# Holding back the first store of an add-and-GELU kernel until chunk 19 is done

## The chip, the cores and the metric

One NeuronCore of a Trainium2 chip. The metric is the device time of one execution in microseconds (us), lower is better. The profile is of one execution; its span is shorter than the timed number by about 1.8 us (119.9 against 121.73 in the execution that was profiled), so spans are compared with spans and times with times. Engines have short names here: POOL is GpSimd, ACT ScalarE, DVE VectorE, and SP is SyncE, which issues the DMA transfers.

## The reference

```python
batch, dim = 1024, 4096                      # float32
z = x + y
return 0.5 * z * (1 + np.tanh(np.sqrt(2 / np.pi) * (z + 0.044715 * z ** 3)))
```

Two inputs of 16.8 MB are read, one output of 16.8 MB is written: 50.33 MB for very little arithmetic.

## The kernel before

On chip the data is one tile `z` of 128 partitions by 32,768 columns. It receives x by DMA; y comes into two rotating buffers of 8,192 columns. The work goes in 32 chunks of 1,024 columns: an addition (POOL, `add`), a square (ACT, `sq`), a multiply-add (DVE, `stt`), a sigmoid (ACT, `sig`) and a product (DVE, `mul`), which puts the result back into `z`. Loads and stores are large, and all are issued from one queue, SP's, with the stores after all loads:

```python
    loads = [2048, 6144, 8192, 8192, 8192]
    stores = [8192, 8192, 8192, 4096, 4096]
    ...
    def store(i):
        a, b = sr[i]
        nc.sync.dma_start(out=ov[:, a:b], in_=zt[:, a:b])
    ...
    def mul(c):
        a, b = cr[c]
        nc.vector.tensor_mul(out=zt[:, a:b], in0=wt[c], in1=zt[:, a:b])

    sp = []
    for i in range(len(loads)):
        sp += [(load_x, i), (load_y, i)]
    sp += [(store, i) for i in range(len(stores))]
    ...
        store: lambda i: [(mul, c) for c in over(cr, *sr[i])],
```

So a store waits for the products of its own columns (the first for chunk 7), and is issued when SP has issued everything ahead of it in this list.

## Time and profile before

| | before |
|---|---|
| time, median of the first three runs | 122.09 us |
| span of the profile | 119.9 us |
| DMA queue busy, share of 16 engines | 98.4% |
| DVE / ACT / POOL busy | 75.5 / 63.8 / 73.0 us |
| first and second store issued | 60.52 and 66.83 us |
| last load lands / last store lands | 80.67 / 119.67 us |

Two more belong here. The first is SP's line in the view of waits (what waited, for whom: us in total, times, the longest), the second the timeline of SP from 60.6 to 67.5 (start, duration, what):

```profile
SPq L131 <- DVE z L157: 41.8, 4, 19.4
```

A landing is the issue's start plus the time to landing of the DMA view. "Landing" is of the last of the 16 DMA engines. A DMA engine moves a transfer in packets, here mostly of 32 KB and 1.21 us each. The packet records behind the DMA view give start, duration and size, but not the engine. They show that the packets of an engine follow each other without a gap while it has work, so the last two load packets of the 16 engines are the last 32 of the load.

### The profile page before, as it was taken

What the parts mean: (1) busy time and instruction counts of PE and PEld (TensorE: products, weight loads), DVE (VectorE), ACT (ScalarE), POOL (GpSimd) and SP (SyncE); (2) the same over time, 40 slices, a digit from 0 to 9 for tenths busy, and PEclk for the clock granted to TensorE, in tenths of its full rate; (3) what the DMA queues carried; (4) which work ended last, traced back from release to release, by engine and by line L of the source; (5) the groups of instructions that cost most, each with busy time, mean ns of one, the idle gap of its engine ahead of it and who ended that gap; (6) DMA issues with size and microseconds to landing.
All of it is one profiled execution on the core that took longest, in us unless ns stands there. A gap on an engine that the chain in (4) does not pass through costs nothing.

```text
span 119.9 us, 247 instructions
## 1 busy us (share of the span) xinstructions
DVE 75.5 (63%) x66; ACT 63.8 (53%) x66; POOL 73.0 (61%) x35
## 2 busy tenths in 40 slices
DVE  0044700049999109999996999996899999600000
ACT  4006300078876038788867887884888887200000
POOL 0046000699990199999969999959999991000000
DMA  6999999989898999999898989999998989998995
GB/s 191 424 478 410 476 426 394 514 361 514 361 503 372 481 394 448 426 426 448 383 492 372 503 350 514 361 383 481 388 481 372 492 383 481 394 470 366 437 426 224
DMA packets 2162, 50.35 MB, mean 420 GB/s; under 512 B 240, under 2 KB 240, under 8 KB 240
## 3 DMA queue, kind: packets, MB, share of 16 engines
q1 hardware_dynamic: 2160, 50.33, 98.4%
q14 instruction: 2, 0.02, 0.0%
HBM read 33.55 MB, written 16.78 MB: 420 GB/s over the span
## 4 chain that ended last, share of the span: by engine, by line
DMA 49%; POOL 17%; DVE 16%; SPq 1%; ACT 1%; issue 0%; POOLq 0%
DMA y<-in_y_dram 49%; POOL z L137 17%; DVE z L157 8%; DVE w L148 8%; ACT w L142 1%; SPq L120 1%; SPq L127 1%; POOLq L137 0%
## 5 line engine op out<-in xcount | busy, mean ns | idle before, releaser
L137 POOL TENSOR_TENSOR z<-z,y 128x1024 f32<-128x1024 f32 x31 | 72.8, 2388 | 26.1 <-DMA y<-in_y_dram 26.1
L142 ACT ACTIVATE w<-z 128x1024 f32<-128x1024 f32 x32 | 32.9, 1028 | 37.3 <-POOL z L137 31.3
L148 DVE SCALAR_TENSOR_TENSOR w<-w,z 128x1024 f32<-128x1024 f32 x32 | 39.4, 1233 | 21.0 <-ACT w L142 21.0
L157 DVE TENSOR_TENSOR z<-w,z 128x1024 f32<-128x1024 f32 x32 | 38.8, 1215 | 0.0
L153 ACT ACTIVATE w<-w 128x1024 f32<-128x1024 f32 x32 | 31.4, 981 | 0.4 <-DVE w L148 0.4
L137 DVE TENSOR_TENSOR z<-z,y 128x1024 f32<-128x1024 f32 x1 | 1.2, 1226 | 6.1 <-DMA y<-in_y_dram 6.1
L196 ACT ACT_TABLE_LOAD x1 | 1.3, 1283 | 1.3 <-PEq L228 1.3
L195 DVE MEMSET one<- 128x1 f32 x1 | 0.1, 59 | 1.3 <-PEq L228 1.3
L228 POOL MEMSET const-float32-0.0<- 128x1 f32 x1 | 0.1, 98 | 0.2 <-issue 0.2
L196 ACT ACTIVATE one<-one 128x1 f32<-128x1 f32 x1 | 0.2, 203 | 0.0
L228 POOL MEMSET const-bfloat16-1.0<- 128x1 bf16 x1 | 0.1, 101 | 0.0
L228 POOL MEMSET const-uint8-127<- 128x1 uint8 x1 | 0.1, 101 | 0.0
L228 POOL MEMSET const-float32-1.0<- 128x1 f32 x1 | 0.1, 98 | 0.0
## 6 DMA issues: line engine op xcount, KB each, us to landing
z<-in_x_dram SPq DMA_DIRECT2D x3, 4096.0 KB, 34.2
y<-in_y_dram SPq DMA_DIRECT2D x3, 4096.0 KB, 24.8
out_dram<-z SPq DMA_DIRECT2D x3, 4096.0 KB, 30.2
out_dram<-z SPq DMA_DIRECT2D x2, 2048.0 KB, 17.3
z<-in_x_dram SPq DMA_DIRECT2D x1, 3072.0 KB, 13.4
y<-in_y_dram SPq DMA_DIRECT2D x1, 3072.0 KB, 20.4
z<-in_x_dram SPq DMA_DIRECT2D x1, 1024.0 KB, 4.9
y<-in_y_dram SPq DMA_DIRECT2D x1, 1024.0 KB, 7.0
```

What stands on the lines that cost most here:

```text
L120: nc.sync.dma_start(out=zt[:, a:b], in_=xv[:, a:b])
L127: nc.sync.dma_start(out=yt[s][:, o : o + b - a], in_=yv[:, a:b])
L137: eng.tensor_add(out=zt[:, a:b], in0=zt[:, a:b], in1=yt[s][:, o : o + b - a])
L142: nc.scalar.activation(out=wt[c], in_=zt[:, a:b], func=act.Square, scale=root)
L148: nc.vector.scalar_tensor_tensor(out=wt[c], in0=wt[c], scalar=c1, in1=zt[:, a:b], op0=alu.add, op1=alu.mult)
L153: nc.scalar.activation(out=wt[c], in_=wt[c], func=act.Sigmoid)
L157: nc.vector.tensor_mul(out=zt[:, a:b], in0=wt[c], in1=zt[:, a:b])
L195: nc.vector.memset(one, 0.0)
L196: nc.scalar.activation(out=one, in_=one, func=act.Sigmoid)
L228: nc = _bacc.Bacc("TRN2", target_bir_lowering=False, num_devices=1)
```

## The change

The intent: stores should not join the queue while loads are still the more urgent work. The first store (and with it all that follow) now waits for the product of chunk 19 as well, which is done near the end of the last load.

```diff
     loads = [2048, 6144, 8192, 8192, 8192]
+    FIRST = 19
...
     def store(i):
         a, b = sr[i]
-        nc.sync.dma_start(out=ov[:, a:b], in_=zt[:, a:b])
+        ins = nc.sync.dma_start(out=ov[:, a:b], in_=zt[:, a:b])
+        if i == 0:
+            tc.add_manual_dep(
+                ins.ins,
+                muls[FIRST].name,
+                mybir.DependencyInfo(mybir.DependencyClass.Sync, mybir.DependencyReason.DATA),
+                reason="the stores join the queue when the last load is nearly done",
+            )
...
-        nc.vector.tensor_mul(out=zt[:, a:b], in0=wt[c], in1=zt[:, a:b])
+        muls[c] = nc.vector.tensor_mul(out=zt[:, a:b], in0=wt[c], in1=zt[:, a:b]).ins
...
-        store: lambda i: [(mul, c) for c in over(cr, *sr[i])],
+        store: lambda i: [(mul, c) for c in over(cr, *sr[i])] + [(mul, FIRST)],
```

More of the change, by code (lines that the diff above doesn't have):

```diff
@@ L115 @@
     zt = pool_sb.tile([P, TOT], fp32, tag="z", name="z")
-    yt, wt = {}, {}
+    yt, wt, muls = {}, {}, {}
     def load_x(i):
```

## The prediction

> **What bounds the kernel now.** I read the page first: busy shares, the DMA queues, then the chain.
>
> ```profile
> span 119.9 us, 247 instructions
> DVE 75.5 (63%) x66; ACT 63.8 (53%) x66; POOL 73.0 (61%) x35
> ...
> DMA packets 2162, 50.35 MB, mean 420 GB/s; under 512 B 240, under 2 KB 240, under 8 KB 240
> ...
> q1 hardware_dynamic: 2160, 50.33, 98.4%
> ...
> DMA 49%; POOL 17%; DVE 16%; SPq 1%; ACT 1%; issue 0%; POOLq 0%
> ```
>
> No compute engine is busy for more than 63% of the span, and the one data queue (all loads and stores are issued by SP) keeps the 16 DMA engines busy for 98.4% of it. The chain (last line) seems to say otherwise, with a third of the span on POOL and DVE. But that chain is followed back from the last compute, which ends at 104; it doesn't say what fills the 16 us after it. So next I asked when each transfer lands. From the DMA view, one issue at a time, with the start of each issue from the timeline of SP:
>
> ```profile
> z<-in_x_dram SPq DMA_DIRECT2D x1, 4096.0 KB, 34.2
> y<-in_y_dram SPq DMA_DIRECT2D x1, 4096.0 KB, 20.6
> out_dram<-z SPq DMA_DIRECT2D x1, 4096.0 KB, 30.2
> out_dram<-z SPq DMA_DIRECT2D x1, 4096.0 KB, 33.5
> out_dram<-z SPq DMA_DIRECT2D x1, 2048.0 KB, 15.7
> ```
>
> These are the last x load (issued 36.41), the last y load (60.09), the first store (60.52), the second store (66.83) and the last store (103.97). Adding, they land at 70.6, 80.7, 90.7, 100.3 and 119.7. Two things are to be seen. They land in the order of issue, 9.6 to 10.1 us apart for each 4 MB, however long before they were issued. And the first store, though issued at 60.5, lands only 10.0 us after the last load: it stood in the queue behind the loads for some 20 us. I then took the four stretches between those landings (the bounds 60.86, 70.57, 80.67, 90.70, 100.36 are landing times); the columns are start:end, length, busy time and count of DVE, ACT, POOL, the TensorE clock, DMA share, GB/s:
>
> ```profile
> 60.86:70.57 9.71, 8.79 (x9) 7.28 (x9) 9.58 (x5) 1.00 1.00 432
> 70.57:80.67 10.10, 10.10 (x10) 8.64 (x10) 8.94 (x4) 1.00 1.01 415
> 80.67:90.70 10.03, 8.74 (x8) 7.23 (x8) 9.89 (x5) 1.00 0.99 426
> 90.70:100.36 9.66, 9.66 (x9) 8.20 (x10) 8.61 (x4) 1.00 1.01 434
> ```
>
> The first row is the last x load, the second the last y load, the third and fourth the first two stores. The DMA engines are full in all four, at 432 and 434 GB/s in undisturbed rows. The second row is the only one of interest: 4 MB took 10.10 us and not 9.71, so 0.39 us is lost as the queue goes from loads to stores. In the packet records the last two packets of that load on each DMA engine, those that start from 76.8 on, last up to 1.87 us instead of 1.21. The third row's 10.03 holds two small instruction fetches and the longer confirmation of a write.
>
> So the bound is the bytes: 50.33 MB at about 433 GB/s is 116.2 us, plus 1.0 us before the first packet, the first transfers' slower start, 0.4 at the turn, and the last confirmation.
>
> **What the Trainium skill says.** "DMA: Bandwidth & Descriptors", section "Where 436 GB/s comes from", gives 435.2 GB/s as the ceiling of the SBUF ports; the rows at 432 and 434 agree, so there is nothing above to reach for. The same page, "Queues, rings and completion order", says that on each DMA engine descriptors are consumed in ring order; the landings above agree. Its section "Anatomy of one DMA" says that DMA engines don't wait on semaphores, the wait is on the issuing sequencer. That makes the question of this change: a wait in front of a store costs time only if the rings run empty meanwhile. And "Latency and other measured facts" gives some 600 ns from an HWDGE issue to the first byte; here the first load is issued at 0.00 (SP is busy with it to 0.38) and the first packet record starts at 1.00, so I use 1.0 us.
>
> **The change, part by part.** The instruction listings of the two kernels agree on DVE, ACT and POOL, in order and in waits; SP has the same 14 rows. Nothing is added or removed. The one change is the value of DVE's semaphore for which SP waits before the first store: the product of chunk 19 (columns 19,456 to 20,479) in place of chunk 7. The second store's own wait for DVE (chunk 15) is dropped, as the first one's covers it.
>
> When is chunk 19 done? The second store needs chunk 15 and is issued at 66.83; the DVE products (line 157) that follow are at 67.88, 70.19, 72.51 and 74.81, so the fourth is chunk 19:
>
> ```profile
> 74.81 1.22 DVE L157 TENSOR_TENSOR z<-w,z 128x1024 f32<-128x1024 f32 x1
> ```
>
> It ends at 76.03. What moves:
> - First store: issued at about 76.07 instead of 60.52, 15.5 us later.
> - Second store: right behind, at about 76.5 instead of 66.83, 9.7 us later.
> - Third, fourth, fifth store: their products end at 86.6, 95.8 and 103.9, as before.
> - Loads: none is behind a store in the queue, so none is issued at another time.
>
> What does it cost? At 76.03 the rings still hold the rest of the last y load: 80.67 - 76.03 = 4.6 us. The first store's packets can begin 1.0 us after issue, at 77.1. So the store is in the rings 3.6 us before it can run (or about 2.9 us before the last load packets end at about 80.0, which is the stricter way to count). The cost on the path is zero. Afterwards two stores of 4 MB are queued, enough until 100.3, and the third joins at 86.6: unchanged from here.
>
> The gain is as small. The loads aren't held up by the queued stores, as they are consumed in order: the rows up to 70.57 run at 432 GB/s with a store queued from 60.5 on. The only thing to gain is the 0.39 us at the turn, if it comes from the stores being fetched too early; and from 77.1 on they are there in the changed kernel too, while in the kernel before the stretching begins at 76.8 to 77.4. At best a fraction, say 0.05 us, I book. Sum: 122.09 - 0.05 = about 122.05 us; the span 119.85.
>
> **The rivals.**
> *A bubble.* The engines run dry between the last load and the first store. For it: the margin of 2.9 to 3.6 us is only some three packets of 1.21 us on each engine, and if an engine looks several packets ahead, a late arrival may cost a part of that. Against: the stretching in the records reaches two packets back, that is 2.4 us, still less than the margin. If chunk 19 were done 1 us later than in this trace nothing would happen; 4 us later would cost about 1 us. It would make 122.3 to 123.
> *The turn gets cheaper.* The 0.39 us are a clash between the load's last packets and the store's first ones. With the store arriving in the midst of these packets, a part or all of it may vanish: 121.7. For it: the stretched packets are those of the load, not of the store. Against: the store is still there before the loads are done, and a turn from reading HBM to writing it remains in any case, once.
> *The last y load lands earlier, and the compute behind it ends earlier.* This is probably the intent: the queue is kept for the loads. For it: POOL waits 1.3 us for that load at 80.67, and the last eight chunks depend on it. Against: the compute's end isn't on the path. The last store is issued at 103.97 and lands 15.7 us later, of which its own 2 MB take about 4.8 (half of 9.66); it stands behind others for over 10 us. Even all 0.39 us earlier it would move nothing but its place in a full queue.
>
> **Range and chances.** The three runs of before lie within 0.02 us, so the range is all from the mechanism: the turn wholly gone (-0.4) to a part of a bubble (+0.4): 121.65 to 122.45. Within 2% means 119.65 to 124.53. To be faster than that, 2.4 us would have to come from a queue that is full at its ceiling rate; what is lost at the turn is a sixth of it: 1%. To be slower takes over 2.4 us of empty rings, so chunk 19 some 5 us later than in this trace: 1%.
>
> **What would show it.** Right: the first two stores issued within 0.5 us of each other at 76 to 76.6; the last y load landing at 80.3 to 80.7, the first store about 10.0 after it; GB/s in the stretch between of 410 to 432; the last store still issued at about 104 and waiting over 10 us; DMA share 98%. Wrong: a slice near 80 with a DMA share well under 0.9; a first store that lands over 10.3 us after the last load; loads before 70 that land at other times than 9.71 us apart (then a queued store does touch loads in front of it); or a first store issued past 78, if chunk 19 is later than in this trace.

## More of the kernel before

```profile
60.52 6.64 SPq L131 DMA_DIRECT2D out_dram<-z  x2
```

SP waits 41.8 us for products of DVE before it issues stores. That looks like an expensive wait, but SP only issues; what it has issued earlier goes on running. The second line joins two stores into one, from the start of the first to the end of the second issue, both well before the last load has landed.

## The result

| | before | changed |
|---|---|---|
| time, median (lowest to highest) | 122.09 us, 6 runs (121.88 to 122.34) | 121.83 us, 6 runs (121.64 to 122.20) |
| ratio | | 0.9984 (95% interval 0.9964 to 1.0003) |
| span of the profile | 119.9 us | 119.9 us |
| first store issued | 60.52 us | 76.11 us |

Ratios are the mean time of one kernel's runs over that of the other's of the same rounds, so not quite the ratio of the medians. This interval covers 1: no difference is shown. The page of the changed kernel answers to the lines shown for before:

```profile
span 119.9 us, 246 instructions
...
DVE 75.5 (63%) x66; ACT 63.8 (53%) x66; POOL 73.0 (61%) x35
...
q1 hardware_dynamic: 2160, 50.33, 98.3%
...
DMA 49%; POOL 17%; DVE 16%; SPq 1%; ACT 1%; issue 0%; POOLq 0%
```

It is the same page within 0.1, with one instruction fewer: SP's wait of its own for the second store is gone, as the prediction has it (the view of SP's store line lists three semaphore instructions in the changed kernel, four before). The change did take place, as SP's waits and its timeline from 60 to 80 (two windows) show:

```profile
SPq L132 <- DVE z L165: 41.7, 4, 15.5
```

```profile
60.15 0.33 SPq L128 DMA_DIRECT2D y<-in_y_dram  x1
...
76.11 0.82 SPq L132 DMA_DIRECT2D out_dram<-z  x2
```

The wait in front of the stores is as long as before in total, 41.7 us: it is only divided otherwise (15.5 and not 19.4 the longest). The first two stores go out together at 76.11, as predicted. And the four stretches between landings, cut as in the prediction (start:end, length, busy time and count of DVE, ACT, POOL, TensorE clock, DMA share, GB/s):

```profile
60.90:70.61 9.71, 8.80 (x9) 7.28 (x9) 9.58 (x5) 1.00 1.00 432
70.61:80.57 9.96, 9.96 (x9) 8.50 (x10) 8.95 (x4) 1.00 1.01 421
80.57:90.71 10.14, 9.00 (x9) 7.48 (x9) 10.01 (x5) 1.00 1.01 435
90.71:100.37 9.66, 9.66 (x10) 8.20 (x10) 8.51 (x4) 1.00 1.01 434
```

The x load takes 9.71 us in both kernels, though before a store was queued behind it for much of that time: the queued store does not hinder loads further ahead. The turn, which is the passage from loads to stores (second row), is 0.14 us shorter than before (10.10), and the next row is 0.11 longer (10.03): the first store lands at 90.71, against 90.70. The small gain of the turn, if it is one, is gone one row later; a landing is that of the slowest of 16 engines, which is now 1.12 us behind the quickest and was 0.95 before. By the median over the engines, the two last loads land 9.96 us apart before and 9.95 after.

### The profile page after: what moved, and what is told of

Read it like the earlier page. It is cut to its first block, busy times and chain, and to the rows that moved or that the text cites. A ratio compares the mean times of both kernels' runs of the same rounds, so it can differ in the third digit from the quotient of the medians.

```text
span 119.9 us, 246 instructions
## 1 busy us (share of the span) xinstructions
DVE 75.5 (63%) x66; ACT 63.8 (53%) x66; POOL 73.0 (61%) x35
## 4 chain that ended last, share of the span: by engine, by line
DMA 49%; POOL 17%; DVE 16%; SPq 1%; ACT 1%; issue 0%; POOLq 0%
DMA y<-in_y_dram 49%; POOL z L145 17%; DVE z L165 8%; DVE w L156 8%; ACT w L150 1%; SPq L121 1%; SPq L128 0%; POOLq L145 0%
## 5 line engine op out<-in xcount | busy, mean ns | idle before, releaser
L156 DVE SCALAR_TENSOR_TENSOR w<-w,z 128x1024 f32<-128x1024 f32 x32 | 39.5, 1233 | 20.9 <-ACT w L150 20.9
```

Of the source, the lines that this page charges most:

```text
L156: nc.vector.scalar_tensor_tensor(out=wt[c], in0=wt[c], scalar=c1, in1=zt[:, a:b], op0=alu.add, op1=alu.mult)
```

## The experiments

The theory: the DMA rings (the queue of packets that waits at each of the 16 DMA engines) are full from the first load to the last store, so moving an issue changes nothing as long as it reaches the rings before they run dry. The rivals: a bubble, that is idle DMA engines, already below that point (the engines need the store some packets ahead); early stores that hinder the loads; the end of the compute as the true bound; and a turn whose cost the late issue can lower. Twelve runs were made, all correct: ten new kernels, one of them twice, and the changed kernel again. Ratios are to runs of the kernel before in the same rounds.

| run | what differs | time, median | ratio to before (95%) |
|---|---|---|---|
| again19 | the changed kernel again | 121.88 | 0.9989 (0.9972 to 1.0006) |
| half, half2 | first store at 77.1 / 77.2 us | 121.38, 121.35 | 0.9945 (0.9928 to 0.9961), 0.9922 (0.9909 to 0.9936) |
| first20 | first store at 78.5 us | 121.72 | 0.9973 (0.9959 to 0.9987) |
| first21 | at 80.5 us | 123.79 | 1.0147 (1.0130 to 1.0164) |
| first23 | at 86.1 us | 128.64 | 1.0549 (1.0529 to 1.0569) |
| act_early | stores on ACT's queue, early | 126.44 | 1.0373 (1.0350 to 1.0395) |
| act_late | stores on ACT's queue, late | 121.51 | 0.9972 (0.9955 to 0.9990) |
| tail3, tail10 | last store about 4 / 13 us later | 121.96, 125.10 | 1.0013 (0.9994 to 1.0032), 1.0263 (1.0239 to 1.0287) |
| turns | first store ahead of the last load in the queue | 122.68 | 1.0050 (1.0034 to 1.0067) |
| warm | 0.5 MB stored at 41 us | 122.17 | 0.9994 (0.9981 to 1.0008) |

### The changed kernel again (again19)

No edit.

> The changed kernel once more, to see whether the 0.26 us between the two medians is more than noise. Theory (the queue is full before and after, only the turn from loads to stores may get cheaper): ratio between 0.997 and 1.000, that is 0 to 0.35 us. Rival (the early stores hindered the loads): the loads before 70 us land closer than 9.71 us apart and the ratio is under 0.997. If the interval covers 1, no difference is shown.

The interval covers 1 again. In its trace the last two loads land 9.96 us apart by the median, 10.14 by the slowest engine. So the shorter turn of the first trace of this kernel (9.96 by the slowest) is not a property of it.

### How late may the store be (first20, first21, first23)

```diff
-    FIRST = 19
+    FIRST = 20        # first20; 21 in first21, 23 in first23
```

> The first store one chunk later, issued at about 78.4 us; with 1.0 us to the first packet it reaches the rings at 79.4, just before the last load packets end at 79.7 to 80.2. Theory (only an empty ring costs): 121.6 to 122.3 us, no bubble, the last load landing at 80.3 to 80.6. Rival (an engine must have the store several packets, 2 to 3 us, ahead): a bubble of 1 us or more, 123 us.

> The first store issued at about 80.7 us, after the last load packet. Theory: the rings are empty from 80.0 to 81.7, so 1.4 to 1.9 us are lost: 123.5 to 124.0 us. The last load then has no store behind it: if the stretched packets come from the store's approach, it lands 9.71 us after the x load, at 80.3; if they come from the load's own end, 10.0 to 10.1 after.

> The first store issued at about 86.65 us, 6.6 us after the last load packet. Theory: one microsecond lost for each microsecond of empty ring, from 80.0 to 87.65: 7.4 to 7.8 us, so 129.5 to 129.9 us. Rival (other slack, such as the 10 us in which the last store stands in the queue, takes a part of the delay up): under 128 us.

first20 shows no bubble, so the rival that wants the store well ahead falls. Its two windows, from the last x to the last y landing and on to the first store's:

```profile
70.66:80.39 9.73, 9.73 (x9) 8.25 (x9) 8.96 (x4) 1.00 1.00 431
80.39:90.72 10.33, 9.44 (x9) 7.92 (x9) 10.20 (x5) 1.00 1.04 446
```

first21 came in at 123.79 us, in the expected range. The same two windows of it, then the DMA busy tenths in 40 slices of 76 to 86 us:

```profile
70.41:80.12 9.71, 9.71 (x9) 8.24 (x9) 8.96 (x4) 1.00 0.88 378
80.12:92.60 12.48, 11.60 (x11) 9.72 (x11) 12.35 (x6) 1.00 0.98 419
```

```profile
DMA  3003900099000000000009600093000930009000
...
q1 hardware_dynamic: 113, 3.18, 74.6%
```

With slices this narrow a packet counts in the slice where it starts, so single zeros between nines mean nothing. The long run of zeros does: in the packet records the last load packets start at about 78.3 and end at 79.6, and the first store's start at 81.4. So the rings are empty for some 1.8 us, and 1.8 us is what the time lost (121.98 to 123.79). Note the first row: with no store behind it, the y load takes 9.71 us, no longer than the x load. So the 0.39 us of before are not the load's own end; they come from the store's presence.

first23 lost 6.7 us where 7.4 to 7.8 were expected, a miss of almost a microsecond. About 0.5 of it is in the issue, at 86.13 and not 86.65, since the last load landed 0.5 us earlier. The rest is in something I had not reckoned with. In each trace there are two fetches of instructions of 8 KB each on the same DMA engines, usually between 83 and 88 us; in before, at 84.56 and 85.92, each takes 0.31 us, and the store packet that starts as it ends takes 1.33 and 1.56 us instead of 1.21. In first23 both fell into the empty stretch. The DMA view of 79 to 87 us of this kernel:

```profile
DMA  0000000010000000000100000000000000000009
...
q14 instruction: 2, 0.02, 0.8%
```

The two ones are the fetches, with nothing beside them. Its 16 engines then finish the last store within 0.17 us of each other, against 0.92 in before. By the median over the engines its last store lands at 126.42 and that of before at 119.12, so 7.30 us are lost, about the time for which the rings were empty (79.7 to 87.0). The other half microsecond is thus most likely this lag that was spared. first21 agrees: its rings ran empty too, but its second fetch, at 86.63, came afterwards, and its engines are 1.10 us apart when the first store lands. No run moved the fetches alone.

### Half a step later (half, half2)

Against the changed kernel, with the recording of `stts` cut:

```diff
-    FIRST = 19
+    FIRST = 21
...
-                muls[FIRST].name,
+                stts[FIRST].name,      # the scalar_tensor_tensor of chunk 21, not a product
...
-        store: lambda i: [(mul, c) for c in over(cr, *sr[i])] + [(mul, FIRST)],
+        store: lambda i: [(mul, c) for c in over(cr, *sr[i])] + [(stt, FIRST)],
```

> The first store half a step later than in the changed kernel: released by chunk 21's scalar_tensor_tensor instead of chunk 19's product, so issued at about 77.25 us and in the rings at 78.25, when the last packets of the last load have just begun. Median over the 16 DMA engines of the time between the last x and the last y landing, so far: 9.96 us with the issue at 60.5, 9.95 at 76.1, 9.73 at 78.5, 9.71 at 80.5 and 86.1. Theory (a store that reaches an engine while it still has load packets to begin stretches them): about 9.75 to 9.9, since only the last packet can be hit; the time 121.6 to 122.1. Rival (what counts is only whether the rings ever run dry): 9.95.

> The fastest kernel so far once more, the first store issued at about 77.2 us, on another set of runs. If the gain is of the turn and not of one chip: ratio 0.993 to 0.997, the last two loads 9.71 to 9.75 us apart, runs within 0.2 us of each other. If it was luck of its four runs: ratio 0.998 to 1.000 as for the changed kernel.

This is the fastest kernel of the study, ahead of the kernel before in both sets of runs, by 0.6 to 0.9 us of the median (122.02 to 121.38, and 122.28 to 121.35). The changed kernel was not run beside it, but the intervals of its ratios (from 0.9964 up) lie above both of these. Not all came as expected: the time of half and the ratio of half2 are below their ranges, and the runs of half2 are 0.6 us apart, not 0.2. SP's timeline and the windows between landings of half:

```profile
77.13 0.82 SPq L132 DMA_DIRECT2D out_dram<-z  x2
```

```profile
60.74:70.47 9.73, 8.83 (x9) 7.32 (x9) 9.59 (x5) 1.00 1.00 431
70.47:80.17 9.70, 9.70 (x9) 8.23 (x9) 8.93 (x4) 1.00 1.00 432
80.17:90.29 10.12, 9.23 (x9) 7.71 (x9) 9.98 (x5) 1.00 0.99 426
90.29:99.95 9.66, 9.66 (x10) 8.19 (x10) 8.54 (x4) 1.00 1.01 434
```

The turn (second row) costs nothing, 9.70 us, and no bubble follows. By the median over engines the last two loads are 9.72 us apart in half and in half2. Both theories in the expectation were too cautious: the cost is not lowered but gone, between an issue at 76.1 (9.95) and one at 77.1 us. In packets: the last two packets of the last load start on each engine at about 77.0 and 78.2. A store that is issued at 76.1, and so in the rings at about 77 (an estimate, from the 0.85 us between issue and first packet in first21), still stretches these two; one issued at 77.1 stretches neither. Counted for all traces, this is the time by which the last two load packets of an engine together exceed twice 1.217 us, as a mean over the 16 engines:

| first store issued | traces | us per engine |
|---|---|---|
| 60.4 to 60.5 us | before, and tail3, tail10 (below; the kernel before up to its last product) | 0.44, 0.51, 0.85 |
| 76.0 to 76.1 us | changed, again19 | 0.28, 0.36 |
| 77.1 us and later | half, half2, act_late, first20, first21, first23 | 0.00 to 0.02 |

So one trace of the kernel before said too little about the size of this cost: in tail3 and tail10 the last two loads land 10.12 and 10.38 us apart by the median, not 9.96.

first20, 1.3 us later, has the free turn too (9.73), but its slowest engine is 1.24 us behind the quickest at the first store, 0.90 in half, and so its span ends at 119.9 again. Whether the ordinary scatter of that lag explains why first20 gained less (0.27%) is not shown. The gains of the four runs with a free turn (0.27% in first20, 0.28% in act_late, 0.55% in half and 0.78% in half2) were measured in four sets of runs on four chips, so they are not compared closely.

The profiled execution of half2 took 121.77 us, its other four runs 121.15 to 121.44. Its trace shows why: the three loads before the last took 9.83, 9.86 and 9.93 us by the median instead of 9.71, so 0.5 us was lost well before any store was issued. What slowed them is not shown. A single profile can miss such a gain.

### Two queues (act_early, act_late)

```diff
-        nc.sync.dma_start(out=ov[:, a:b], in_=zt[:, a:b])
+        nc.scalar.dma_start(out=ov[:, a:b], in_=zt[:, a:b])
...
-    sp += [(store, i) for i in range(len(stores))]
+    after_sig = {15: [0], 17: [1], 25: [2], 29: [3]}   # act_early; act_late: {21: [0, 1], 25: [2], 29: [3]}
...
             acts.append((sig, i))
+            acts += [(store, j) for j in after_sig.get(i, [])]
...
+    acts.append((store, len(stores) - 1))
```

act_early is otherwise the kernel before, act_late the changed one.

> The kernel before with its stores issued from ACT, on a queue of their own, the first two at about 62 and 68 us. Wrong order is now possible: a store can run beside the loads. Theory (on one queue the stores stand behind the loads, so the early issue was harmless; on two queues they share the DMA engines): the last y load, with 18 us of loads left at 62 and two stores beside them, lands at 95 to 100 us instead of 80.7, the compute ends 14 to 19 us later, at 118 to 123, and the time is 125 to 131 us. Rival (the DMA engines serve whatever was issued first, whatever the queue): 122 us as before.

> The changed kernel with its stores issued from ACT, the first two at about 77 us. Theory: at most 3.5 us of the last load are left and are shared with the first store, so the load lands at 83 to 85 us and the compute ends 3 to 4 us later, which the last store's 10 us in the queue take up: 121.7 to 122.6 us. So here, on two queues, the late issue is worth 3 to 9 us against its early twin, while on one queue it was worth nothing. Rival (the queues make no difference): both ACT kernels at 122 us.

On a queue of its own the early store is harmful: 126.44 us, 3.7% over. The chain of waits of act_early has the last y load in one line (start, us, what):

```profile
60.02 34.87 DMA y<-in_y_dram
```

Issued at 60.02, it lands at 94.89 and not at 80.67; from 68 us on the packet records show store packets in between the load packets, one by one. The stretch is there too, though this store has a queue of its own: the two load packets of each engine just ahead of its first store packet, from 64.8 us on, take up to 1.96 us (0.76 us per engine, counted as above). The compute that depends on it ends after 118, the last store is issued at 118.2 and lands at 124.5. The late issue on two queues loses none of it. I had expected 83 to 85 for its last load; it landed at 80.31, and its first store packets, of a store issued at 77.28, start at 79.2, when the load packets end. Its time, 121.51, is below the expected range as well. So the intent behind the change is sound where stores have another queue than loads, and worth 4.9 us there (126.44 to 121.51); with one queue the order of the queue has already done it.

act_late is also a little faster than before (0.9972). Its turn is clean, 9.72 us, which agrees with half.

### The end of the compute (tail3, tail10)

The tile `scr` is new and nobody reads it.

```diff
     def mul(c):
         a, b = cr[c]
+        if c == C - 1:
+            for _ in range(3):           # 10 in tail10
+                nc.vector.tensor_mul(out=scr, in0=wt[c], in1=zt[:, a:b])
```

> The kernel before with three further products of 1.2 us (result unused) ahead of the last product, so that the last store is issued about 3.6 us later, at 107.6. Theory (the end of the compute is not on the path; the last store stands about 10 us in the queue): 122.0 to 122.2 us, as before. Rival (the chain of the page, DVE to the end, is the bound): 3.6 us longer, 125.7 us.

> The same with ten further products, so that the last store is issued about 11.9 us later, at 115.9. Theory: the queue ahead of it (the fourth store's last packet at about 114) has run empty; the store lands 1.0 + 4.9 + 0.7 us after its issue, at 122.4, so 2.7 us are lost: 124.3 to 125.2 us. Rival (DVE is the bound all the way): 134 us.

Both as the theory has it. In tail3 the last store goes out at 107.68, 3.7 us later than before, and the time is the same. In tail10 (SP's timeline, then the DMA view of this issue: KB, us to landing):

```profile
116.93 0.33 SPq L132 DMA_DIRECT2D out_dram<-z  x1
```

```profile
out_dram<-z SPq DMA_DIRECT2D x1, 2048.0 KB, 6.3
```

The store that in before took 15.7 us to land takes 6.3 once the queue ahead of it is empty. So 9.4 us of the 15.7 were standing in line: that is the slack of the compute at the end. The ten products moved its issue by 13.0 us, so 13.0 - 9.4 = 3.6 us should be lost; the time rose by 3.3. This is why an earlier landing of the last load cannot show in the time of the kernel before.

### The price of a turn (turns, warm)

turns puts the first store between the last two loads; warm stores the first chunk alone (0.5 MB) early in the queue.

```diff
     for i in range(len(loads)):
-        sp += [(load_x, i), (load_y, i)]
-    sp += [(store, i) for i in range(len(stores))]
+        sp += [(load_x, i)]
+        if i == len(loads) - 1:
+            sp += [(store, 0)]
+        sp += [(load_y, i)]
+    sp += [(store, i) for i in range(1, len(stores))]
```

```diff
-    stores = [8192, 8192, 8192, 4096, 4096]
+    stores = [1024, 7168, 8192, 8192, 4096, 4096]
...
+        if i == 3:
+            sp += [(store, 0)]
         sp += [(load_x, i), (load_y, i)]
-    sp += [(store, i) for i in range(len(stores))]
+    sp += [(store, i) for i in range(1, len(stores))]
```

> The kernel before with the first store moved ahead of the last y load in the one queue (it is issued at about 39.5 us, the last y load at 60.1 still): three turns between loads and stores instead of one. Theory (each turn from loads to stores with the store queued costs some 0.25 us, and position in the queue, not issue time, sets when a transfer runs): last x load at 70.8 to 71.0, first store at 80.5 to 80.9, last y load at 90.3 to 91, so the compute ends 10 us later, at 113.7 to 114.5, and the last store, with its slack of 10 us used up, just misses its place: 122.5 to 123.6 us. Rival (turns are dear, 1 us or more): the last y load past 91.5 and 124.5 us or more.

> The kernel before with the first chunk's 0.5 MB stored early, in the one queue between the second and the third pair of loads, where it runs at about 41 us; the other stores are issued as before. In the run with three turns only the first meeting of a queued store with load packets stretched those packets (4 MB in 10.36 us), the second did not. Theory A (the stretch is paid once, by the first store that is queued behind loads): the load packets just ahead of 41 us are stretched, and at the turn near 82 us the last y load lands 9.71 to 9.75 us after the last x load; the time as before, 121.7 to 122.2 us, as the cost is only moved. Theory B (the stretch belongs to the turn at which the long run of loads ends with a store queued): the last two loads land 9.95 to 10.15 us apart, and the time is 0.2 to 0.5 us more than before.

The windows of turns between landings (x load, first store, y load, second store):

```profile
60.75:71.11 10.36, 9.45 (x9) 7.95 (x9) 10.22 (x5) 1.00 1.00 405
71.11:80.82 9.71, 9.71 (x10) 8.23 (x10) 8.29 (x4) 1.00 1.00 432
80.82:90.94 10.12, 2.03 (x2) 0.56 (x1) 0.00 (x0) 1.00 1.03 442
90.94:100.62 9.68, 6.12 (x6) 6.08 (x7) 9.55 (x5) 1.00 1.00 433
```

Two things follow. Position in the queue, not the issue time, decides when a transfer runs: the y load, issued at 59.99, waits its turn behind the store and lands at 90.94. And the load packets are stretched at the first turn (10.36 us) but not at the last: in the third row the packet records show the y load's packets at 1.21 us up to the second store, though that one had been queued since 66.7; the row's 10.12 holds the two instruction fetches. (The first store was issued at 47.3 and not at 39.5 as I had written: chunk 7's product comes after a step of chunk 8 on DVE, so it waits for the next load.)

warm then tests whether the cost is paid once, by the first store queued behind loads. Its windows are the y load just ahead of the small store, and later the last x and the last y load:

```profile
31.37:42.12 10.75, 7.76 (x7) 5.55 (x6) 4.31 (x2) 1.00 0.96 372
...
62.80:72.51 9.71, 7.63 (x8) 6.15 (x7) 9.64 (x5) 1.00 1.00 432
72.51:82.24 9.73, 9.73 (x9) 8.27 (x9) 8.88 (x4) 1.00 1.00 430
```

It is: the load ahead of the small store takes 10.75 us, and the turn at 82 is free, with five stores to come and the first of them queued 20 us ahead. The stretch belongs to the first store that has load packets in front of it on the engine (in act_early, in another queue), not to the turn. The time is as before, the cost was only moved. What the DMA engine does in that time (a first access to the output, a first read of the tile, something else) no run here tells, and that stays open.

## Why the prediction was right

The time lay within the stated range, and the steps can be checked one by one.

*The bound.* Right. Bytes at the ceiling rate: 432 and 434 GB/s before and after, 98% busy, and every delay that leaves the rings filled is free (the change itself, first20, tail3), while one that empties them costs what it empties (first21: 1.8 us of empty rings, 1.8 us of time).

*When chunk 19 is done, and what is issued then.* Right: 76.11, with the second store straight behind it, and the last store still at 103.88 with 15.8 us to landing.

*The margin of 2.9 to 3.6 us.* Right in kind: 2.4 us of further delay (first20) made no bubble, 4.4 us (first21) made one. It was a little large: 4.4 us of delay left the rings empty for 1.8, so the margin was 2.6 us, as the load packets end at 79.6 and not at 80.0 when nothing stretches them. The 1.0 us from issue to first packet was somewhat high; first21 shows 0.85 (80.53 to 81.38).

*The 0.05 us booked for a cheaper turn.* Nothing of that size can be shown; the two intervals of this kernel reach from 0.9964 to 1.0006. The packet counts (0.28 and 0.36 us against 0.44 to 0.85) suggest that a part of the cost was saved, more than was booked; with so few traces this is not shown. That the medians are 0.26 us apart is no success of this step. The range was also said to be all from the mechanism, since three runs lay within 0.02 us; all six lie within 0.46 us, which is more than the whole turn was thought to cost.

*The rival "the turn gets cheaper".* This is the step that was judged too low. I held against it that "a turn from reading HBM to writing it remains in any case, once", and that the store would be there before the loads were done. The first is false in these runs: the turn itself is free (9.70 in half, 9.73 in warm), what cost was the first store's arrival behind load packets. The second is true and decides nothing: in half the store is in the rings at about 78.0 by the same estimate, 1.2 us before the first load packets end there (79.2), and the turn is free all the same. What decides is whether it comes 1 us earlier still. The upper bound of 0.39 us drawn from one trace was low too: half gains 0.64 and 0.93 us in its timed medians. The profiled execution of before, at 121.73 us, was quicker than all six that were timed (121.88 to 122.34), and the stretch reaches 0.85 us in tail10, so a gain of about this size fits; no trace of before from the rounds of half was taken to show it.

*The third row's 10.03 us.* One reading of it was wrong: "the longer confirmation of a write" is not what lengthens it. From the end of the last packet to the landing it takes 0.34 us by the median for the first store, 0.30 for the last y load and 0.45 for the last x load.

*The rival of the bubble* fell (first20), and *the rival of the compute's end* fell (tail3, tail10). The intent of the change was met in neither kernel, as the loads were never held up: with one queue they could not be, with two they are (act_early).

## What to carry to other kernels

When all transfers go through one queue and it never runs dry, the time of an issue is almost free to choose; look for the moment at which the queue would be empty and for what stands ahead, not at the length of the issuer's wait. If stores have a queue of their own, their issue time decides how much they take from the loads, and holding them back can be worth several per cent (4% here). A small stretch in one row between landings is worth an experiment in half-steps: here an issue at 76.1 gained nothing that could be shown, one at 77.1 or 77.2 gained over 0.5%, and one at 80.5 lost 1.5%.

## What the Trainium skill lacked or had wrong

- "DMA: Bandwidth & Descriptors", section "Queues, rings and completion order", has the order of the rings right (turns: a load issued at 59.99 behind a store landed at 90.94). It does not say that the first store of a program, if it is queued while load packets are still to begin, stretches these packets: 0.25 to 0.66 us by the median landings in before, tail3 and tail10, 10.75 us instead of 9.71 for the load ahead of the small store in warm, and also from a second queue (act_early); at later turns, or with the first store issued 3 us before the last load landed (half), nothing.
- The same section says that engines go round-robin between queue rows, by packets. act_early agrees: from 68 us on a store packet and a load packet take turns. What the page says in "Issuing engines are not separate DMA queues", that several issuing engines only save issue time, needs a warning beside it: the same stores on a second queue brought the last load from 80.67 to 94.89 us and the time to 126.44.
- The same page, "Latency and other measured facts", gives about 600 ns from an HWDGE issue to the first byte, and not from which moment it counts. From the start of the issue to the first packet record it was 1.00 us for the first load and 0.85 us for a store into empty rings (first21); from the end of the issue, 0.62 and 0.50 us, so the figure fits if it is counted from there.
- No page has the effect of instruction fetches on a full DMA queue: two of 8 KB each took 0.31 us and stretched the store packets behind them from 1.21 to 1.33 and 1.56 us (before); in first23, where they fell into empty rings, the 16 engines finished within 0.17 us of each other instead of 0.92.
